# The passage between two layers of a hybrid mixer kernel, put in another order: output product by token tile, modulation and gates moved, copies shared

## Chip, cores and metric

One core of one Trainium2 chip. The metric is the device time of one execution in microseconds (us); several runs are taken and their median stands for a kernel.

## What is computed

Two trunk layers over 256 latent tokens `x` and 256 context tokens `ctx` of width 1024, float32. In each layer both streams are RMS-normalised and modulated (scale and shift from a conditioning vector), go through one wide input projection, then through three parallel token mixers (a bidirectional RWKV-7 recurrence, neighbourhood attention, differential attention), each with a SiLU gate; the branches are projected, weighted by sigmoid gates and summed, and an output projection follows. Its rows are normalised and added to the stream. In the last layer the context only serves as keys and values, so its rows need no gates and no output.

```
for l in range(DEPTH):
    mod_x = silu(c) @ w_mod[l] + b_mod[l]          # shift, scale, gate; mod_c likewise
    hx  = rmsnorm(x,  g_pre[l]) * (1 + sc_x) + sh_x
    hcn = rmsnorm(hc, g_pre[l]) * (1 + sc_c) + sh_c
    y_x, y_c = mixer(hx, hcn, w_in[l], ...)        # ends with  sum(gb * yb) @ w_out
    x  = x  + gt_x * rmsnorm(y_x, g_post[l])
    hc = hc + gt_c * rmsnorm(y_c, g_post[l])       # not in the last layer
```

## The kernel before

Tokens come in four tiles of 128: tiles 0 and 1 are `x`, tiles 2 and 3 the context. A float32 product is made of three products of float32r parts (`mm3`, high x high, high x low, low x high); weights arrive in 256 KB chunks on SP's DMA queue (`chunk`), ScalarE makes the high part `wh` and VectorE the remainder `wl` (`split`). Nearly all instructions go through helpers, so lines such as L195 (matmul), L199 (transpose), L164 (activation), L185, L189 and L192 (VectorE), L167 (DMA) stand for many places, and the tiles' names tell them apart: `z`, `a`, `b`, `y` are PSUM tags, `k` is the general pool of 52 slots of 128x512, `wr`/`wh`/`wl` weights, `gs` staging.

The order of instructions on each engine is chosen when the program is built: a scheduler goes through the program in its order as priority, with modelled durations, and emits what it takes to be ready; a slot is given when the first writer of a tile is emitted. `keep_in_program_order` pins an instruction behind everything ahead of it on its engine.

The passage from layer 0 to layer 1:

- `outproj` (L1272): for each of four column chunks `c` of 256, four weight chunks `kh`; for each, all four token tiles. When a chunk is done, each tile's PSUM is read twice: a Square on ScalarE for the norm's sum (`gs`), a product with the gate row on VectorE (`y`). `ahead` loads the old rows and, from the fifth step on, up to 15 of the 32 modulation chunks (`in_wm`).
- `residual` (L1302): one reduction and one inverse root (`rsqrt`, L201, Newton steps on VectorE) for all four tiles, then eight residual rows (L192, 128x512); tiles 0 and 1 go out to DRAM `xd` on POOL's queue, for the next layer's residual.
- `start` (L449): `norm_rows` for tiles 0 and 1, then 2 and 3 (two Squares a row, a root for each pair, scaling in place); for each of eight channel blocks `k` four transposes into `b`, a copy to `ht`. The modulation (`mod_rows`, L378) is a generator: four groups `g` of 32 small products `y<-k,cs` with 128x32 tiles, then a transpose into `z` and the scales and shifts `mA`, `mB` of two channel blocks. The loop over `g` modulates two blocks, splits them into the parts `h`, and lets weight chunks of input columns 6, 2 and 4 run on them for all 512 tokens. Then `derived` (small parameters), column chunk 0 for the x tokens, and the RWKV stage.
- `run` (L1317) weaves the recurrence (`rwkv`) with filler (`zs`: gates, further input columns) by the costs and debts in `yl`; layer 1's gates of the first branch come first in that filler.

In the RWKV stage `rwkv_inv` (L777) inverts 128 triangular blocks of 64x64: VectorE inverts the 32x32 diagonal blocks, turns the result once for each of `RA` and `RB` (`X<-X`), ScalarE copies the four turned quadrants to `Lab`, and TensorE makes the off-diagonal blocks with two passes of 32x32 products (`a<-X,Lab`, then `a<-X,k`), alternating between the two directions `d`, each direction in a block of its own of the array. It is done four times, twice in each layer.

Of the kernel before, what the change touches and what calls it, by code (L numbers as in the profile page):

```python
# [10 lines left out]
F32 = mybir.dt.float32  # L11
# [123 lines left out]
class K:  # L135
# [65 lines left out]
    def rsqrt(self, v, n, scale, eps, op=ALU.add, rows=128):  # L201

        a, b, y, t = (self.small(n) for _ in range(4))
# [158 lines left out]
    def mod_rows(self, l, P, ws):  # L362
# [9 lines left out]
        for g in range(4):  # L372
            for k in range(8):
                for i in range(4):
                    ins = self.mm(mp[32 * i:32 * i + 32, g, :], self.cs[:, k].rearrange("p a b -> p (a b)"),
                                  ws[8 * g + k][:, 128 * i:128 * i + 128], k == 0, k == 7)
# [72 lines left out]
    def start(self, l, P, xs, mod, ws, nr=T):  # L449

        self.in_order = l == 0
# [3 lines left out]
        for _ in range(8 if l == 0 else 0):  # L455
            next(mod)
# [29 lines left out]
        r = self.now(self.z_pair(l, 0, 0, nr))  # L486
        self.have["rx", l, 0] = True
        self.have["rz", l, 0] = row[0], self.rwkv_rows(l, P, 0, 1, r, 0, nr, nr == T) or [None, None], row[1]
# [288 lines left out]
    def rwkv_inv(self, e):  # L777
# [169 lines left out]
    def gates(self, l, n, b):  # L947

        for g in range(2):
# [322 lines left out]
    def outproj(self, l, s, ns, ss, ahead):  # L1272

        G = [self.gate_rows(l, st) for st in range(ns)]
        y = []
        for t in range(2 * ns):
            yt = self.k4.tile([128, 2, 512], F32, tag="k4", name=f"y{self.count()}")
            y.append([yt[:, 0, :], yt[:, 1, :]])
        for c in range(4):
            p = [self.ps("za"[c % 2], (128, 2, 256)) for _ in range(ns)]  # L1280
            for kh in range(4):
                w = self.split(self.io["wo"][l, c, kh])
                ahead(4 * c + kh)
                for t in range(2 * ns):
                    for k in range(2):
                        kk = 2 * kh + k
                        self.mm3(p[t // 2][:, t % 2, :], [a[:, 128 * t:128 * t + 128] for a in s[kk]],
                                 [a[:, k, :] for a in w], kk == 0 and t % 2 == 0, kk == 7 and t % 2 == 1)
            cs = slice(256 * (c % 2), 256 * (c % 2) + 256)
            for t in range(2 * ns):  # L1290
                pt = p[t // 2][:, t % 2, :]
                self.act(self.stage(256), pt, AF.Square, accum_out=ss[:, 4 * t + c:4 * t + c + 1])
                self.tt(y[t][c // 2][:, cs], pt, G[t // 2][c // 2][:, cs], ALU.mult)
        return y

    def rows_load(self, src, t, xs):

        xs.append([self.slot(), self.slot()])
        for j in range(2):
            self.dma(self.nc.sync, xs[t][j], src[128 * t:128 * t + 128, 512 * j:512 * j + 512])  # L1300

    def residual(self, y, ss, xs, last):  # L1302
        n = len(y)
        s2 = self.small(n)
        self.red(s2, ss.rearrange("p (t j) -> p t j", j=4), ALU.add)
        rs = self.rsqrt(s2, n, 1.0 / 1024, RMS_EPS)
        for t in range(n):
            for j in range(2):
                rows = slice(128 * t, 128 * t + 128)
# [163 lines left out]
```

## Time and profile before

| | us |
|---|---|
| median of three runs | 1433.27 |
| lowest, highest | 1431.86, 1433.60 |
| the profiled execution | 1431.83 |
| its span, first to last instruction | 1430.0 |
| mean granted TensorE clock, of full speed | 0.964 |

The profile is of one execution. Engines: PE is TensorE, PEld its weight loads, DVE VectorE, ACT ScalarE, POOL GpSimd, SP the engine that only issues DMAs here. A row of the timeline has start, duration, engine, line, operation, output<-input, count, and in brackets how long the engine was idle before and which engine and tile ended that. Ends of matmuls are modelled; the distance between starts is what they cost. PEclk 1.00 is 2.4 GHz, 0.50 the lower level of 1.2 GHz. A row of stages has the stretch and its length, busy time (and instructions) of PE, PEld, DVE, ACT and POOL, then PEclk, the busy share of the DMA engines and what they moved in GB/s.

### The profile page before, as it was taken

The page shows a single profiled execution, that of the slowest core. Times are in us where ns is not written, and L with a number is a line of the kernel's source. Part 1 is how long each engine was busy: PE and PEld are TensorE (multiplying, and loading weights), DVE is VectorE, ACT ScalarE, POOL GpSimd, SP SyncE. Part 2 cuts the span into 40 slices and gives each one's busy share as a digit, 9 for nine tenths or more (in the row PEclk, how much of TensorE's full clock was granted, in tenths as well). Part 3 has the DMA queues.
Part 4 walks back from the last instruction along what each step waited for, and adds up shares of the span by engine and source line. Part 5 has one row for each costly group of instructions (what it writes and reads, how often), then busy time and mean ns, then how long its engine had stood idle before and what let it go on. Part 6 is the DMA issues. An engine that isn't in the chain of part 4 may idle for free. (4 is left out here: it accounts for less than half of the span.)

```text
span 1430.0 us, 28585 instructions
## 1 busy us (share of the span) xinstructions
PE 1314.2 (92%) x10784; PEld 1097.1 (77%) x10784; DVE 973.4 (68%) x2047; ACT 811.5 (57%) x1750; POOL 234.6 (16%) x292
## 2 busy tenths in 40 slices
PE   6998999899998999999899969998999999989796
PEld 4865777788777876677778958887888789867686
DVE  4763469726887367768675367768837892689886
ACT  5462375545964436667533355766558736567653
POOL 0010011003110012223235001011111000022441
PEclk9999999999998999999999989999989999999998
DMA  9466642324314268422533943553613242685454
GB/s 357 125 202 191 201 137 81 118 77 143 124 62 124 64 172 236 150 97 81 199 127 122 315 156 107 186 173 115 188 61 97 75 140 69 196 266 169 130 163 148
DMA packets 112986, 212.42 MB, mean 149 GB/s; under 512 B 13088, under 2 KB 24880, under 8 KB 112848
## 3 DMA queue, kind: packets, MB, share of 16 engines
q1 hardware_dynamic: 102896, 178.33, 39.4%
q0 software_dynamic: 9952, 32.26, 6.8%
q8 instruction: 85, 1.39, 0.4%
q14 instruction: 53, 0.43, 0.1%
HBM read 176.70 MB, written 33.83 MB: 147 GB/s over the span
## 5 line engine op out<-in xcount | busy, mean ns | idle before, releaser
L195 PE MATMUL z<-k,wh 128*128 128x512 f32 (+1 forms) x2288 | 633.5, 360 | 9.5 <-ACT wh L164 5.7
L195 PEld LDWEIGHTS z<-k,wh 128*128 128x128 f32 x2288 | 406.3, 194 | 75.7 <-issue 9.4
L195 PE MATMUL z<-k,wl 128*128 128x512 f32 (+1 forms) x1144 | 408.2, 359 | 8.6 <-DVE wl L185 8.6
L164 ACT ACTIVATE wh<-wr 128x512 fp32r<-128x512 f32 x376 | 234.2, 630 | 296.8 <-PE z L195 175.9
L185 DVE TENSOR_TENSOR wl<-wr,wh 128x512 fp32r<-128x512 f32 x376 | 280.3, 752 | 170.6 <-PE z L195 70.8
L195 PEld LDWEIGHTS z<-k,wl 128*128 128x128 f32 x1144 | 221.2, 194 | 41.8 <-DVE wl L185 12.8
L195 PE MATMUL z<-wh,k 128*128 128x256 f32 x704 | 140.3, 293 | 1.5 <-ACT k L164 1.3
L195 PEld LDWEIGHTS z<-wh,k 128*128 128x128 f32 x704 | 115.5, 198 | 3.5 <-ACT k L164 1.5
L185 POOL TENSOR_TENSOR k<-k,k 64x512 fp32r<-64x512 f32 (+3 forms) x64 | 78.4, 1231 | 168.5 <-ACT k L164 88.3
L195 PE MATMUL z<-wl,k 128*128 128x256 f32 x352 | 102.7, 292 | 1.6 <-DVE wl L185 1.5
L164 ACT ACTIVATE gs<-z 128x512 f32<-128x512 f32 (+1 forms) x132 | 66.1, 501 | 63.7 <-PE z L195 54.1
L164 ACT ACTIVATE k<-k 64x256 fp32r<-64x256 f32 (+5 forms) x154 | 79.4, 541 | 29.7 <-POOL k L185 21.8
L185 DVE TENSOR_TENSOR k<-k,k 128x256 f32<-128x256 f32 (+5 forms) x126 | 79.5, 644 | 17.8 <-ACT k L164 14.6
L199 PE MATMUL b<-cst,k 128*128 128x128 f32 x384 | 67.5, 292 | 21.0 <-ACT k L164 4.8
L199 PEld LDWEIGHTS b<-cst,k 128*128 128x128 f32 x384 | 45.2, 147 | 42.5 <-issue 14.0
L164 ACT ACTIVATE k<-a,s 128x512 f32<-128x512 f32 (+1 forms) x96 | 59.1, 616 | 32.5 <-DVE s L179 31.9
L164 ACT ACTIVATE k<-b 128x256 f32<-128x256 f32 (+1 forms) x152 | 67.3, 471 | 16.9 <-PE b L199 16.0
L195 PE MATMUL a<-k,k 128*128 128x512 f32 (+1 forms) x192 | 61.0, 399 | 12.5 <-ACT k L164 10.2
L195 PEld LDWEIGHTS z<-wl,k 128*128 128x128 f32 x352 | 69.6, 198 | 2.8 <-DVE wl L185 2.3
L195 PE MATMUL a<-ar,bk 64*128 64x128 f32 (+1 forms) x512 | 49.9, 285 | 10.0 <-ACT Lab L164 9.3
L195 PEld LDWEIGHTS a<-ar,bk 64*128 64x128 f32 x512 | 42.4, 187 | 21.7 <-ACT Lab L164 16.3
L179 DVE TENSOR_REDUCE s<-a 128x1 f32<-128x512 f32 (+1 forms) x96 | 56.4, 587 | 1.7 <-PE a L195 1.7
(169 smaller groups left out, 1948.8 us busy)
## 6 DMA issues: line engine op xcount, KB each, us to landing
wr<-in_wi SPq DMA_DIRECT2D x296, 256.0 KB, 3.0
k<-in_wm SPq DMA_DIRECT2D x64, 256.0 KB, 5.4
wr<-in_wb SPq DMA_DIRECT2D x48, 256.0 KB, 2.6
md<-gs SPq DMA_DIRECT2D x36, 256.0 KB, 2.7
k<-md POOLq DMA_DIRECT2D x36, 256.0 KB, 4.3
wr<-in_wg SPq DMA_DIRECT2D x32, 256.0 KB, 2.9
wr<-in_wo SPq DMA_DIRECT2D x32, 256.0 KB, 3.9
gd<-gs SPq DMA_DIRECT2D x18, 256.0 KB, 3.0
```

Of the source, the lines that this page charges most:

```text
L164: return self.nc.scalar.activation(out=out, in_=in_, func=func, **kw)
L179: return self.nc.vector.tensor_reduce(out=out, in_=in_, axis=AX.X, op=op, **kw)
L185: return (eng or self.nc.vector).tensor_tensor(out=out, in0=a, in1=b, op=op)
L195: return self.nc.tensor.matmul(out, lhsT=lhsT, rhs=rhs, start=start, stop=stop)
L199: return self.nc.tensor.transpose(out, in_, self.ident[0:k, 0:k])
```

## The change

- `rsqrt` with one value per partition uses eight VectorE instructions in place of eleven.
- In the last column chunk `outproj` goes by token tile: all four weight chunks for tile 0, then tile 1 and so on. After each tile's reads it calls `done`, which runs residual and norm for that tile alone; in layer 0 tiles 2 and 3 are put off.
- The modulation's products stand between the projection's steps (two pieces after each step from the eighth on), their chunks are loaded earlier, and their pin is gone.
- `start_next` takes the place of `start` in layer 1: x's rows are transposed, modulated out of PSUM and split (`stream_in`), column chunk 0 and the gates of branch 0 run on the x tokens, between them the context tiles' residual and norm, then the context's stream and column chunks 6, 2 and 4.
- In `rwkv_inv` the first pass goes direction by direction, and two of the four copies to `Lab` are made by VectorE after each half of it.

```diff
     def rsqrt(self, v, n, scale, eps, op=ALU.add, rows=128):
+        if n == 1:
...
+            self.ts(t, y, y, a, ALU.mult, ALU.mult)
+            self.ts(b, t, -10.0 / 3.0, t, ALU.add, ALU.mult)
+            self.ts(y, b, 5.0, y, ALU.add, ALU.mult)
...
     def mod_rows(self, l, P, ws):
-                    if l and g == k == i == 0:
-                        self.tc.keep_in_program_order(ins)
...
+    def stream_in(self, P, hn, s):
+        c = slice(256 * s, 256 * s + 256)
+        for k in range(8):
+            p = self.ps("b", (128, 256))
+            self.turn_rows(hn, k, p)
+            t = self.slot((128, 256))
+            A, B = P["A"][:, s, k:k + 1], P["B"][:, s, k:k + 1]
+            self.ts(t, p, A, B, ALU.mult, ALU.add)
+            self.act(self.h[0][k][:, c], p, AF.Identity, scale=A, bias=B)
+            self.tt(self.h[1][k][:, c], t, self.h[0][k][:, c].bitcast(F32), ALU.subtract)
+
+    def norm_row(self, x):
+        ss = self.small(2)
+        for j in range(2):
+            self.act(self.stage(512), x[j], AF.Square, accum_out=ss[:, j:j + 1])
+        s2 = self.small(1)
+        self.red(s2, ss, ALU.add)
+        rs = self.rsqrt(s2, 1, 1.0 / 1024, RMS_EPS)
+        self.act(x[0], x[0], AF.Copy, scale=rs)
+        self.ts(x[1], x[1], rs)
+
+    def start_next(self, l, P, nr, ctx):
+        r = self.now(self.z_pair(l, 0, 0, nr))
+        self.rwkv_rows(l, P, 0, 1, r, 0, nr, False)
+        ctx[0]()
+        self.now(self.gates(l, nr, 0))
+        ctx[1]()
+        self.rwkv_wa(l, P, self.now(self.z_pair(l, 6, 0, T)), 0, T)
+        row = [self.rwkv_rows(l, P, 0, w, self.now(self.z_pair(l, c, 0, T)), 0, T, True) for w, c in ((0, 2), (2, 4))]
...
     def rwkv_inv(self, e):
+        def diag(d, q, copy):
+            R, r = RA if d == 0 else RB, rows(d, q)
+            copy(Lab[r, :, 32 * q:32 * q + 32], R[r].rearrange("p t k -> p k t"))
         for hf in range(2):
             QQ = self.ps("a", (128, 16, 32))
-            for k in range(16):
-                for d in range(2):
-                    rs, ra, cs = off(d)
-                    N = RB if d == 0 else RA
+            for d in (1, 0):
+                rs, ra, cs = off(d)
+                N = RB if d == 0 else RA
+                for k in range(16):
                     self.mm(QQ[ra, k, :], Lab[rs, 16 * hf + k, cs], N[rs, :, 16 * hf + k])
             q = self.slot((128, 16, 32))
+            self.act(q[64:96], QQ[64:96])
             self.act(q[32:64], QQ[32:64])
-            self.act(q[64:96], QQ[64:96])
             Qs.append(q)
+            diag(hf, 0, self.cp)
             yield self.yl[e["l"]]["q"][e["sg"]]
         for d in range(2):
-            R = RA if d == 0 else RB
-            for q in range(2):
-                r = rows(d, q)
-                self.act(
-                    Lab[r, :, 32 * q:32 * q + 32], R[r].rearrange("p t k -> p k t"))
+            diag(d, 1, self.act)
...
     def outproj(self, l, s, ns, ahead, done):
+            if c < 3:
+                pp = [self.ps("za"[c % 2], (128, 2, 256)) for _ in range(ns)]
+                p = [pp[t // 2][:, t % 2, :] for t in range(n)]
+            else:
+                p = [self.ps("aazz"[t], (128, 256)) for t in range(n)]
...
+            ws = []
             for kh in range(4):
+                ws.append(self.split(self.io["wo"][l, c, kh]))
                 ahead(4 * c + kh)
+                for t in range(n if c < 3 else 1):
+                    part(ws[kh], kh, t)
+            for t in range(n):
+                if c == 3 and t:
+                    for kh in range(4):
+                        part(ws[kh], kh, t)
+                read(t)
+                if c == 3:
+                    done(t, y[t], ss[t])
...
     def run(self):
                 def zs():
-                    yield from self.gates(l, nq, 0)
+                    if l == 0:
+                        yield from self.gates(l, nq, 0)
...
+                    self.derived(l + 1, PN)
+                    self.h_new()
                     mod = self.mod_rows(l + 1, PN, ws)
                 def ahead(i):
-                    if not last and i >= 4:
-                        self.mod_load(l + 1, ws, i)
+                    if not last:
+                        self.mod_load(l + 1, ws, 2 * i - 4)
+                        for _ in range(2 if i > 6 else 0):
+                            next(mod)
+                def rows(t, y, ss):
+                    self.residual(t, y, ss, xs[t], last)
+                    if not last:
+                        self.norm_row(xs[t])
+                def done(t, y, ss):
+                    if t < 2:
+                        rows(t, y, ss)
+                    else:
+                        late.append((t, y, ss))
+                self.outproj(l, s, 1 if last else 2, ahead, done)
                 if not last:
-                    next(mod)
-                self.residual(y, ss, xs, last)
-                if not last:
-                    self.start(l + 1, PN, xs, mod, ws, NX)
+                    self.mod_load(l + 1, ws, 32)
+                    self.now(mod)
+                    self.stream_in(PN, xs[0:2], 0)
+                    self.start_next(l + 1, PN, NX, (lambda: [rows(*a) for a in late],
+                                                    lambda: self.stream_in(PN, xs[2:4], 1)))
```

## Rows read from the trace of the kernel before

**Rows 1.** The page, part 1: busy time, share of the span, instructions.
```profile
PE 1314.2 (92%) x10784; PEld 1097.1 (77%) x10784; DVE 973.4 (68%) x2047; ACT 811.5 (57%) x1750; POOL 234.6 (16%) x292
```

**Rows 2.** Busy time by stage: projection, passage, part of it, after; last stage; second inversion.
```profile
786.00:823.00 37.00, 37.00 (x319) 36.87 (x321) 14.66 (x29) 13.71 (x42) 1.61 (x3) 1.00 0.89 310
822.60:846.90 24.30, 12.53 (x164) 9.01 (x162) 16.62 (x63) 15.63 (x41) 2.73 (x5) 0.72 0.43 149
...
835.00:845.00 10.00, 7.15 (x28) 4.89 (x29) 5.74 (x19) 5.74 (x10) 0.00 (x0) 0.50 0.07 26
...
846.90:884.00 37.10, 37.08 (x274) 30.31 (x275) 22.08 (x53) 15.62 (x32) 1.08 (x2) 1.00 0.38 128
...
1280.00:1430.00 150.00, 125.61 (x905) 113.47 (x904) 119.52 (x263) 85.58 (x208) 45.54 (x53) 0.94 0.49 159
458.50:474.00 15.50, 15.45 (x297) 15.07 (x298) 1.26 (x2) 12.20 (x15) 0.00 (x0) 0.64 0.12 33
```

**Rows 3.** What TensorE waited for, whole span: us in total, times, longest.
```profile
PE a L195 <- ACT k L164: 16.3, 13, 3.6
...
PE a L195 <- DVE X L182: 9.3, 3, 5.8
...
PE z L199 <- DVE k L185: 6.0, 2, 5.3
```

**Rows 4.** Groups by line and shape, 822.6 to 846.9: busy us, mean ns, idle before.
```profile
L199 PE MATMUL b<-cst,k 128*128 128x128 f32 x32 | 7.8, 415 | 4.5 <-ACT k L164 4.5
...
L164 ACT ACTIVATE gs<-k 128x512 f32<-128x512 f32 x8 | 5.0, 631 | 1.5 <-DVE k L192 1.5
...
L189 DVE TENSOR_SCALAR k<-k,mA,mB 128x256 f32<-128x256 f32 x8 | 2.9, 408 | 2.2 <-ACT k L164 2.1
...
L185 DVE TENSOR_TENSOR wl<-wr,wh 128x512 fp32r<-128x512 f32 x1 | 0.7, 691 | 0.3 <-PE a L195 0.3
```

**Rows 5.** Timeline of TensorE: transposes of the passage; a modulation group among products.
```profile
840.53 5.14 PE L199 MATMUL b<-cst,k 128*128 128x128 f32 x24 [0.47 <-ACT k L164]
...
854.99 0.39 PE L195 MATMUL b<-k,wl 128*128 128x512 f32 x1
855.31 1.95 PE L195 MATMUL y<-k,cs 128*32 128x128 f32 x64
...
857.76 0.39 PE L195 MATMUL z<-k,wl 128*128 128x512 f32 x1
```

**Rows 6.** Timeline of the projection: a weight load and products on the same rows.
```profile
821.50 0.19 PEld L195 LDWEIGHTS a<-wl,k 128*128 128x128 f32 x1
...
821.73 0.40 PE L195 MATMUL a<-wh,k 128*128 128x256 f32 x2
...
821.97 0.28 PE L195 MATMUL a<-wl,k 128*128 128x256 f32 x1
```

**Rows 7.** Tile `xd`: time of its transfers from issue to landing.
```profile
DMA to landing us min/median/max: 4.8/5.6/6.1
```

**Rows 8.** Tile `X` of the inversions: ns min/median/max, first and last start.
```profile
L195 PEld LDWEIGHTS a<-X,Lab x512: 101/121/152, 275.0 to 1183.5; 32*32 32x32 f32 x171
...
L164 ACT ACTIVATE Lab<-X x16: 1910/1942/2193, 272.7 to 1184.6; 32x1024 f32<-32x1024 f32 x16
L182 DVE STREAM_TRANSPOSE X<-X x8: 1236/1568/2151, 271.4 to 1177.9; 128x1024 f32<-128x1024 f32 x8
```

**Rows 9.** Timeline of TensorE, first inversion: its first pass of small products.
```profile
274.95 3.80 PE L195 MATMUL a<-X,Lab 32*32 32x32 f32 x128
```

**Rows 10.** Timeline of VectorE at the kernel's end.
```profile
1420.56 0.42 DVE L185 TENSOR_TENSOR y<-a,k 128x256 f32<-128x256 f32 x1 [4.36 <-ACT gs L164]
...
1421.52 0.42 DVE L185 TENSOR_TENSOR y<-a,k 128x256 f32<-128x256 f32 x1 [0.54 <-ACT gs L164]
1421.86 0.15 DVE L179 TENSOR_REDUCE s<-s 128x2 f32<-128x8 f32 x1
...
1423.83 2.74 DVE L192 SCALAR_TENSOR_TENSOR k<-y,s,k 128x512 f32<-128x512 f32 x4
```

More of the change, by code (lines that the diff above doesn't have):

```diff
@@ L201, in rsqrt @@
     def rsqrt(self, v, n, scale, eps, op=ALU.add, rows=128):
+        if n == 1:
+            a, b, y, t = (self.small(1) for _ in range(4))
+            self.ts(a, v, scale, eps, ALU.mult, op)
+            self.ts(y.bitcast(I32), a.bitcast(I32), -0.5, float(0x5F3759DF), ALU.mult, ALU.add)
+            self.ts(t, y, y, a, ALU.mult, ALU.mult)
+            self.ts(b, t, -10.0 / 3.0, t, ALU.add, ALU.mult)
+            self.ts(y, b, 5.0, y, ALU.add, ALU.mult)
+            self.ts(t, y, y, a, ALU.mult, ALU.mult)
+            self.ts(t, t, -0.5 * 0.375 ** 3, 1.5 * 0.375, ALU.mult, ALU.add)
+            self.tt(y, t, y, ALU.mult)
+            return y
         a, b, y, t = (self.small(n) for _ in range(4))
@@ L454, in start @@
         ht = []
-        for _ in range(8 if l == 0 else 0):
+        for _ in range(8):
             next(mod)
@@ L485, in start @@
         row = [self.rwkv_rows(l, P, 0, w, p[c], 0, T, True) for w, c in ((0, 2), (2, 4))]
-        r = self.now(self.z_pair(l, 0, 0, nr))
+        r = self.now(self.z_pair(l, 0, 0, T))
         self.have["rx", l, 0] = True
-        self.have["rz", l, 0] = row[0], self.rwkv_rows(l, P, 0, 1, r, 0, nr, nr == T) or [None, None], row[1]
+        self.have["rz", l, 0] = row[0], self.rwkv_rows(l, P, 0, 1, r, 0, T, True) or [None, None], row[1]
     def stage(self, n):
@@ L945, in gate_load, with gates @@
         return t
-    def gates(self, l, n, b):
-        for g in range(2):
+    def gates(self, l, n, b, gs=range(2)):
+        for g in gs:
             p = yield from self.z_pair(l, (7, 15, 23)[b] + g, 0, n)
@@ L1270, in merged, with outproj @@
         return s
-    def outproj(self, l, s, ns, ss, ahead):
+    def outproj(self, l, s, ns, ahead, done):
         G = [self.gate_rows(l, st) for st in range(ns)]
-        y = []
-        for t in range(2 * ns):
+        n = 2 * ns
+        y, ss = [], [self.small(4) for _ in range(n)]
+        for t in range(n):
             yt = self.k4.tile([128, 2, 512], F32, tag="k4", name=f"y{self.count()}")
@@ L1279, in outproj, with part, read @@
         for c in range(4):
-            p = [self.ps("za"[c % 2], (128, 2, 256)) for _ in range(ns)]
+            cs = slice(256 * (c % 2), 256 * (c % 2) + 256)
+            if c < 3:
[3 more added lines that the diff above has]
+                p = [self.ps("aazz"[t], (128, 256)) for t in range(n)]
+            def part(w, kh, t):
+                for k in range(2):
+                    kk = 2 * kh + k
+                    self.mm3(p[t], [a[:, 128 * t:128 * t + 128] for a in s[kk]], [a[:, k, :] for a in w],
+                             kk == 0 and (c == 3 or t % 2 == 0), kk == 7 and (c == 3 or t % 2 == 1))
+            def read(t):
+                self.act(self.stage(256), p[t], AF.Square, accum_out=ss[t][:, c:c + 1])
+                self.tt(y[t][c // 2][:, cs], p[t], G[t // 2][c // 2][:, cs], ALU.mult)
+            ws = []
             for kh in range(4):
-                w = self.split(self.io["wo"][l, c, kh])
+                ws.append(self.split(self.io["wo"][l, c, kh]))
                 ahead(4 * c + kh)
[L1284 to L1294, printed above, removed]
+                for t in range(n if c < 3 else 1):
+                    part(ws[kh], kh, t)
+            for t in range(n):
+                if c == 3 and t:
[4 more added lines that the diff above has]
+                    done(t, y[t], ss[t])
     def rows_load(self, src, t, xs):
@@ L1299, in rows_load, with residual @@
         for j in range(2):
[L1300 to L1309, printed above, removed]
-                xo = xs[t][j]
-                self.stt(xo, y[t][j], rs[:, t:t + 1], xo, ALU.mult, ALU.add)
-                if last:
-                    self.dma(self.nc.sync, self.out[rows, 512 * j:512 * j + 512], xo)
-                elif t < 2:
-                    self.dma(self.nc.gpsimd, self.xd[rows, 512 * j:512 * j + 512], xo)
+            self.dma(self.nc.sync, xs[-1][j], src[128 * t:128 * t + 128, 512 * j:512 * j + 512])
+    def residual(self, t, y, ss, xs, last):
+        s2 = self.small(1)
+        self.red(s2, ss, ALU.add)
+        rs = self.rsqrt(s2, 1, 1.0 / 1024, RMS_EPS)
+        for j in range(2):
+            rows = slice(128 * t, 128 * t + 128)
+            xo = xs[j]
+            self.stt(xo, y[j], rs, xo, ALU.mult, ALU.add)
+            if last:
+                self.dma(self.nc.sync, self.out[rows, 512 * j:512 * j + 512], xo)
+            elif t < 2:
+                self.dma(self.nc.gpsimd, self.xd[rows, 512 * j:512 * j + 512], xo)
     def run(self):
```

12 lines of the change are left out of this document (6 added, 6 removed).

## The prediction, made before the changed kernel was run

> **What bounds the kernel now.** I read the page's busy times first: TensorE is busy for 92% of the span, far ahead of VectorE and ScalarE [rows 1]. So time is to be had where TensorE stands idle or runs slowly, and a table of stages shows where that is. Between the last product of layer 0's output projection (822.6 us) and the first input product of layer 1 (846.9 us) it is busy for 12.5 of 24.3 us at a granted clock of 0.72, while the stages on both sides leave it no gap [rows 2]. The list of waits names what it stands for: VectorE's results `k` ahead of the modulation's turning [rows 3]; the transposes there run with a granted clock of 0.50, the lower level of 1.2 GHz, in the stretch from 835 to 845 us [rows 2]. This is the chain residual, norm, transpose, modulation; each link waits for all four token tiles.
>
> Of the 24.3 us, real work is small. Two modulation groups take 1.95 each [rows 5] (3.9). The 32 transposes took 7.8 [rows 4], nearly all at the lower level, so 3.9 at 2.4 GHz. **About 16.5 us are waste, and that is the most the passage can give.** What follows it (144 products of 512 columns, two more groups, 48 products of 256 columns) is packed and stays.
>
> **The passage, step by step.** Products of 256 columns come 0.12 apart [rows 6], so a token tile's last columns take 24 x 0.12 = 2.9, and after tile 1 (the second of the x rows) TensorE still has 5.8 us of tiles 2 and 3.
>
> Row chain of tile 1. At the kernel's end the same steps show: second read 0.96 after the first, 1.97 from the reduction to the first residual row, 0.68 per residual row [rows 10]. With one read and three inverse-root steps less (0.2 each, 1.97 over ten) the first residual starts some 2.6 us after the tile's last product. The first half goes out to `xd` at about 3.4, and the norm scales these rows in place, so it waits for that write to have landed: 5.6 more [rows 7], 9.0, and 0.7 for the scaling: 9.7. The arithmetic beside it (two squares of 0.63 [rows 4] and what reads their sums, a second inverse root of 1.8) ends at about 7.7 and is not the last; the write is, on POOL's queue, behind nothing else. Cover: 5.8 of products, and the two modulation groups left after the projection, 3.9: also 9.7. I take 1 us of idling (0 to 6).
>
> x's stream. Per 128 channels VectorE does one modulation (0.41 [rows 4]) and one subtraction (0.42, the nearest being the read in [rows 10]): 6.6 for eight, and up to two weight remainders of 0.69 [rows 4], 8. TensorE has 16 transposes (1.9) and 48 products (5.8), 7.7. With the lag at both ends 2 us idle (1 to 4).
>
> Context rows. Their residuals, norms and stream (VectorE about 16 us: four residual rows, two scalings, two inverse-root chains, 6.6 of stream, beside twelve weight remainders, 8.3, and the gates' and the first rows' own steps) have only the gates' 96 products as cover, 11.5 us, and what is done before. I take 3 (0 to 8). On SP's queue the gates' eight weight loads and two stores now stand ahead of the weights of chunks 6, 2 and 4: 2.6 MB, 8.5 us at 310 GB/s [rows 2], under 11.5 of products. A lowered clock after these gaps costs 1 (0 to 2). Waste left: 7 (1 to 20).
>
> Modulation between the projection's steps. One group among the products cost 2.77 from 854.99 to 857.76 for three products of 0.227 and 64 records at 0.0277: some 0.3 for entering and leaving [rows 5]. Eighteen pieces in nine steps instead of four groups: up to 14 x 0.3 = 4.2 more, at least nothing; I take 2.5. The passage gives 16.5 - 7 - 2.5 = **7.0** (15.5 to -8).
>
> Removed at no price: the pin of the first modulation product, the copies of the turned rows (ScalarE, off the path once the streams take their place). `derived` moves ahead of the projection: a dozen VectorE steps of 0.16 and one POOL load, under TensorE's full stage; without that cover 2 us.
>
> **The end of the kernel.** Tile 0's read, root and residual go beside tile 1's 2.9 us of products. Saved [rows 10]: a read 0.96, two residual rows 1.37, three steps 0.6. I take **2.5** (1 to 3); two output writes follow as before.
>
> **The four block inversions.** TensorE waits 9.3 us in three of them for VectorE's turned inverse [rows 3]; one turning takes 1.57 [rows 8]. The direction that needs only the first one now goes ahead, up to 1.57 each, 4.7 together. Then ScalarE spends four copies of 1.94 in a row [rows 8], and in the first inversion TensorE waits 3.6 us [rows 3] for the results queued behind them. Two go to VectorE, which is busy for 1.3 of 15.5 us in the second inversion [rows 2], so I cost them at nothing; without that cover it is 8 copies x 2 us, and the weight remainders queued behind them would make TensorE late. What is late next is ScalarE's other two copies. Gain without the reordering's price: 6 (0 to 10).
>
> The reordering's price. The small products alternate between two blocks of the array now, 3.80 us for 128 records, 29.7 ns each [rows 9]; after, sixteen in a row use one block. No row shows that. From below: transposes of 128 columns at full clock take 0.107 (an estimate: half of the 0.21 apart at which 24 of them ran at the lower level [rows 5]), 32 columns a quarter, 27 ns, so pairing hardly helps today and nothing is lost, or a little gained. From above: the load of such a block lasts 121 ns [rows 8]; if no load hides, 4 x 128 x 91 ns = 47 us. The nearest row is the projection, where loads of 0.19 us into the very rows in use lie under products 0.12 apart [rows 6], so loads do hide. I take 34 ns: 2 us in all. Net gain **4** (10 to -2, without the upper end, which is a rival).
> The Trainium skill, *TensorE: Matmul & The Clock Gate*, "The mechanism" (Part 3), speaks against this step: weight loads overlap running products only when their row groups differ. By it the sum would carry the 47 us. The trace disagrees for the whole array [rows 6] and shows nothing for one block.
>
> **Layer 1 after the passage.** The gates' 11.5 us of products are gone as filler for its recurrent part, so the interleaving draws later chunks earlier and leaves less for the attention. There TensorE is busy 125.6 and VectorE 119.5 of the last 150 us [rows 2]: filler is short. I take a loss of **1** (4, or a gain of 2).
>
> **Sum.** The profiled execution took 1431.83 (span 1430.0): 1431.8 - 7.0 - 2.5 - 4 + 1 = 1419.3. The median of the runs is 1.4 above it, so the forecast is **1421**, its own range 1412 to 1430.
>
> **Rivals.**
> *The covers all hold.* For it: both sides of the passage are packed, and the chain and its cover come out equal. Passage 13, end 3, inversions 8: 1433.3 - 24 = 1409. Against: everything must fit at once.
> *Loads become the bound.* During the projection the DMA engines are busy for 89%, at 310 GB/s, TensorE never waiting [rows 2]. The change wants 16 more modulation chunks of 256 KB by the same point, 4.2 MB, 13.5 us at that rate, against some 8 us of added TensorE time: 5.6 late; and the output weights stand behind them in SP's queue, perhaps 3 more. The passage gives nothing: 1428 to 1430.
> *Nothing moves.* The order on each engine is fixed when the program is built, from modelled times. If modulation products are put where their chunks have not landed, TensorE waits inside the projection for what it saves behind it: 1433.
> *Slower: one block at a time costs its loads.* It decides in the inversions, at the first product passes, from 29.7 ns a record: the gain is eaten at 27 ns more (14 us over 512 records), 57 ns. At 75 ns it is 1442, at the full 121 ns 1466. For it: nothing shows unpaired blocks. Against: loads under products [rows 6], and 27 ns being the stream itself.
>
> **How the numbers follow.** Forecast 0.60, covers hold 0.16, loads 0.09, nothing 0.06, slower 0.09. About 0.2% (2.9 us) is what a measurement of this kernel can tell from no change. Faster: 0.60 + 0.16 + 0.07 of the loads case = 0.83; same 0.08; slower 0.09. The range 1406 to 1432 leaves out the slower case, half of "nothing" and a few hundredths below.
>
> **What would show it.** Right: from the last projection product to the first input product of layer 1 some 8 to 12 us with two modulation groups and 16 transposes in it, TensorE's wait there naming DMA `xd` or VectorE; the stretch at the lower clock gone; at the end, two residual rows after the last product instead of four; in the inversions no 3.6 us wait, first pass 3.8 to 5 us, ScalarE two copies. Wrong: waits of TensorE or ScalarE on DMA `in_wm` or `in_wo` inside the projection; a first pass of over 7 us; the sum of idling in layer 1 after 900 us grown by more than 4.

## The result and the profile after

The changed kernel takes 1446.49 us (median of 6 runs, 1440.75 to 1448.24) beside 1432.94 for the kernel before: 1.0091 of its time, 95% interval 1.0067 to 1.0115. It is slower by 13 us where 12 less were forecast. The profiled execution took 1448.16 (span 1446.5). Part 1 of its page, against [rows 1]: TensorE has the same 10,784 records and is busy 22 us longer.

```profile
PE 1336.3 (92%) x10784; PEld 1115.0 (77%) x10784; DVE 990.9 (69%) x2109; ACT 795.3 (55%) x1742; POOL 234.9 (16%) x292
```

Where the time went is read by setting equal events of the two timelines side by side (starts, us):

| event | before | after | difference |
|---|---|---|---|
| first small products of the second inversion | 458.5 | 455.5 | -3.0 |
| second operand's wait (1.28) early in the projection | 784.9 | 788.1 | +3.2 |
| last product of the projection | 822.45 | 839.21 | +16.8 |
| layer 1's fourth group of recurrent products `a<-ar,bk` (waits 0.37 us for `Lab`) | 962.0 | 978.6 | +16.5 |
| first small products of the fourth inversion | 1179.9 | 1194.4 | +14.5 |
| last product | 1419.7 | 1437.3 | +17.6 |
| end | 1430.0 | 1446.5 | +16.5 |

So the inversions start early and end late, the projection loses 13.6 us, the stretch behind it gives nothing back (although two modulation groups, 128 records, have moved out of it into the projection), and the end gains 1.1.

**Inversions.** TensorE's timeline in the second one (start, duration, operation, count of records, idle time before):

```profile
455.54 3.82 PE L195 MATMUL a<-X,Lab 32*32 32x32 f32 x64 [5.02 <-DVE X L182]
460.44 3.81 PE L195 MATMUL a<-X,Lab 32*32 32x32 f32 x64
```

64 records of one block take 3.82 us; alternating, 128 took 3.80 [rows 9]. The starts of the single records in the two traces show more than these sums. In one block a record starts every 57 ns (median). In the alternating pass of the kernel before every second start is 57 ns after the one before last as well, and another lies in between, so that they are 28 apart on average: a block is no faster there, two blocks work side by side. The rows of tile `X` (min/median/max ns) show that the copies were no loss: ScalarE keeps eight, VectorE's eight take about half of a ScalarE copy's time. The loads' median does not tell the two orders apart: among the runs below it is 122 ns with one block at a time (`inv_only`) and 141 alternating (`pass_only`).

```profile
L195 PEld LDWEIGHTS a<-X,Lab x512: 101/141/152, 274.2 to 1201.0; 32*32 32x32 f32 x171
...
L164 ACT ACTIVATE Lab<-X x8: 1921/1952/2202, 271.9 to 1196.9; 32x1024 f32<-32x1024 f32 x8
L176 DVE COPY Lab<-X x8: 976/1022/1035, 273.7 to 1197.0; 32x1024 f32<-32x1024 f32 x8
```

**Passage.** Stages of the changed kernel (columns as in [rows 2]): the projection, a part of it, what stands in place of the old gap, and the products put ahead (the image's first input products and gates, which the change puts in front of the context's).

```profile
786.30:839.40 53.10, 47.12 (x441) 43.11 (x441) 22.23 (x71) 17.45 (x53) 5.59 (x8) 0.94 0.84 297
818.00:824.00 6.00, 5.01 (x28) 4.40 (x29) 2.24 (x6) 2.00 (x8) 0.00 (x0) 0.50 1.04 382
839.40:850.40 11.00, 7.06 (x138) 5.34 (x137) 9.40 (x41) 5.19 (x17) 1.08 (x2) 0.75 0.44 145
850.40:882.60 32.20, 25.62 (x158) 23.71 (x156) 22.75 (x64) 15.39 (x33) 0.49 (x1) 0.82 0.31 92
```

The gap of 24.3 us is 11.0 now, as forecast. But the products put ahead (144 products 0.12 apart, 17 us) take 32.2 at a granted clock of 0.82, and the projection 53.1. At the lower level such products come 0.21 apart; a clock of 0.82 is 11.6 of the 32.2 us at that level, worth up to 5 us (an estimate from these three numbers). TensorE's long waits there, from its timeline:

```profile
818.99 0.47 PE L199 MATMUL z<-cst,k 128*128 128x128 f32 x1 [4.46 <-DVE k L185]
...
843.73 0.33 PE L199 MATMUL z<-cst,k 128*128 128x128 f32 x1 [1.99 <-DVE k L185]
...
878.04 0.51 PE L195 MATMUL z<-k,wh 128*128 128x256 f32 x2 [2.83 <-DVE gs L192]
...
884.34 0.44 PE L199 MATMUL b<-cst,k 128*128 128x128 f32 x2 [1.67 <-ACT k L164]
885.90 0.69 PE L199 MATMUL b<-cst,k 128*128 128x128 f32 x2 [1.13 <-ACT k L164]
```

The first is a modulation group's turning. VectorE's timeline shows why it is late:

```profile
816.03 0.69 DVE L185 TENSOR_TENSOR wl<-wr,wh 128x512 fp32r<-128x512 f32 x1 [1.33 <-ACT wh L164]
818.04 0.69 DVE L185 TENSOR_TENSOR wl<-wr,wh 128x512 fp32r<-128x512 f32 x1 [1.33 <-ACT wh L164]
818.65 0.28 DVE L185 TENSOR_TENSOR k<-y,k 128x128 f32<-128x128 f32 x1
```

The row addition (818.65) stands behind two remainders of the last columns' weights, which wait for ScalarE's rounding, and that waits for the chunk: ScalarE stood 14.2 us for DMA `in_wo` from 786 to 840 us. In the kernel before it stood 12.1 us there, and TensorE not at all. What differs is that the last four chunks are rounded 2.0 us apart for 1.4, while the first token tile of the last columns uses one up in six products, 0.7 us. TensorE itself is at 1.2 GHz (0.50) in the stretch from 818 to 824 us, just after having stood. The wait of 2.83 us is of the same kind. VectorE's read of a gate's product (877.56) stands behind two of the context's residual rows and behind a sum that waits for ScalarE's squares:

```profile
875.08 1.42 DVE L192 SCALAR_TENSOR_TENSOR k<-y,s,k 128x512 f32<-128x512 f32 x2
877.29 0.15 DVE L179 TENSOR_REDUCE s<-s 128x1 f32<-128x2 f32 x1 [0.80 <-ACT gs L164]
...
877.56 0.42 DVE L192 SCALAR_TENSOR_TENSOR gs<-gs,z 128x256 f32<-128x256 f32 x1
```

### The profile page after: what moved, and what is told of

The parts are those of the page before. It is cut to its first block, busy times and chain, and to the rows that moved or that the text cites. A ratio compares the mean times of both kernels' runs of the same rounds, so it can differ in the third digit from the quotient of the medians.

```text
span 1446.5 us, 28636 instructions
## 1 busy us (share of the span) xinstructions
PE 1336.3 (92%) x10784; PEld 1115.0 (77%) x10784; DVE 990.9 (69%) x2109; ACT 795.3 (55%) x1742; POOL 234.9 (16%) x292
## 4 chain that ended last, share of the span: by engine, by line
PE 59%; DVE 17%; ACT 10%; DMA 7%; issue 5%; POOL 1%; SPq 1%; DVEq 0%; ACTq 0%; POOLq 0%
PE z L195 37%; PE a L195 12%; ACT k L164 6%; PE y L195 5%; DVE wl L185 4%; PE b L199 3%; DVE k L185 3%; PE b L195 3%; DMA wr<-in_wi 2%; DMA k<-in_wm 2%; DVE k L192 2%; DVE X L182 2%; ACT wh L164 1%; DVE s L179 1%; DVE X L185 1%
## 5 line engine op out<-in xcount | busy, mean ns | idle before, releaser
L195 PE MATMUL z<-k,wh 128*128 128x512 f32 (+1 forms) x2352 | 656.0, 362 | 11.4 <-ACT wh L164 5.1
L195 PEld LDWEIGHTS z<-k,wh 128*128 128x128 f32 x2352 | 419.6, 194 | 80.3 <-issue 9.2
L195 PE MATMUL z<-k,wl 128*128 128x512 f32 (+1 forms) x1176 | 422.3, 361 | 11.7 <-DVE wl L185 11.7
L195 PEld LDWEIGHTS z<-k,wl 128*128 128x128 f32 x1176 | 227.7, 194 | 47.0 <-DVE wl L185 17.0
L195 PE MATMUL z<-wh,k 128*128 128x256 f32 x736 | 148.7, 297 | 1.5 <-ACT k L164 1.3
L195 PEld LDWEIGHTS z<-wh,k 128*128 128x128 f32 x736 | 122.8, 202 | 4.3 <-ACT k L164 1.5
L195 PE MATMUL z<-wl,k 128*128 128x256 f32 x368 | 108.7, 296 | 1.7 <-DVE wl L185 1.5
L185 DVE TENSOR_TENSOR k<-k,k 128x256 fp32r<-128x256 f32 (+5 forms) x134 | 81.0, 614 | 17.8 <-ACT k L164 14.5
L164 ACT ACTIVATE k<-k 64x256 fp32r<-64x256 f32 (+5 forms) x146 | 74.7, 537 | 29.5 <-POOL k L185 21.9
L195 PEld LDWEIGHTS z<-wl,k 128*128 128x128 f32 x368 | 74.3, 202 | 2.7 <-DVE wl L185 2.3
```

The lines of the kernel that those rows point to most:

```text
L164: return self.nc.scalar.activation(out=out, in_=in_, func=func, **kw)
L185: return (eng or self.nc.vector).tensor_tensor(out=out, in0=a, in1=b, op=op)
L195: return self.nc.tensor.matmul(out, lhsT=lhsT, rhs=rhs, start=start, stop=stop)
```

## Experiments

Ratios are to the kernel before, timed together with each batch (medians 1431.38, 1432.07, 1432.61, 1433.88 and 1431.87 us); kernels of different batches are compared by them, with 0.001 taken as 1.43 us. "Stage A" is from the 1.28 us wait to the projection's last product, "stage B" from there to the fourth group of recurrent products of the table above (before: 37.5 and 139.6 us; the changed kernel: 51.1 and 139.3). Each was read in one profiled execution; where TensorE stands for nothing, stage A is 37.5 us at a granted clock of 1.00 (before, `tail_paired`) and 39.0 at 0.96 (`inv_paired`, `tiles_old`), so 1.5 us of it are the clock.

**The two halves.** `inv_only` is the kernel before with the new inversion, `pass_only` the changed kernel with the old one, and `inv_paired` and `after_paired` have the new inversion with the blocks alternating again:

```
-            for d in (1, 0):
-                ...
-                for k in range(16):
+            for k in range(16):
+                for d in (1, 0):
+                    ...
```

> The kernel before with the new block inversion alone. Theory B (one block of the array at a time makes each record of the first product pass cost 60 ns in place of 30): four first passes of 6.8 to 7.6 us in place of 3.8, partly offset by ScalarE's two copies less: 1437 to 1441. Rival (the inversion helps as forecast and the whole loss is the passage): 1427 to 1431, first passes near 4 us.

> As inv_only, but the first pass alternates between the two blocks as before; two copies on VectorE stay. Theory B: first passes back at 3.8 us, the copies' gain left alone: 1426 to 1432, 7 to 12 us under inv_only. Rival (the VectorE copies cost, not the order): within 2 us of inv_only.

> The changed kernel with the old block inversion. Theory L (16 more modulation chunks during the output projection saturate the DMA engines, so an output weight chunk comes late, VectorE stands in its queue on it, and TensorE waits for the modulation's turning): projection from its first to its last product 50 us or more in place of 39.4, and 1438 to 1444. Rival (the loss is the inversion's): 1421 to 1428.

> The changed kernel with only the alternation put back in the first pass. Theory B: 6 to 10 us under the changed kernel, 1436 to 1441, still over before by what the passage costs. Rival (order of blocks does not matter): 1445 to 1448.

`inv_only` 1439.44 us, 1.0048 (1.003 to 1.0067); `inv_paired` 1423.30, 0.9934 (0.9911 to 0.9957); `pass_only` 1442.86, 1.0082 (1.0057 to 1.0107); `after_paired` 1430.90, 0.9994 (0.9975 to 1.0013). Both halves lose. The order of the two blocks alone costs 16.1 us: shown. 512 records at 29 ns more are 14.8, and 13.0 us of it lie, in the two traces, between the first product of the first pass and the first of the second, summed over the four inversions. With it undone the inversion gains 9.5 us (0.0066 of 1432). That puts `inv_paired` below the range expected for it, as `after_paired` is, 14 us under the changed kernel by the ratios. In `inv_paired` four records run between the two turnings, the rest of the pass is as dense as before, and the wait for the results behind the copies, 3.6 us in the first inversion, is down to 1.14:

```profile
279.63 3.81 PE L195 MATMUL a<-X,k 32*32 32x32 f32 x128 [1.14 <-ACT k L164]
...
451.84 0.41 PE L195 MATMUL a<-X,Lab 32*32 32x32 f32 x4 [5.03 <-DVE X L182]
454.40 3.81 PE L195 MATMUL a<-X,Lab 32*32 32x32 f32 x124
```

The passage with the tail costs 8.6 us (0.0060) beside the paired inversion, 11.7 beside the old one. The rest is about these.

**Modulation and loads in the projection**, all from `after_paired`: `mod_late` takes the products out (`next(mod)` in `ahead` deleted), `mod_half` loads every second chunk only (it leaves out half of the modulation's weights), `turn_late` leaves the products and puts row additions and turnings behind the projection.

```
 def mod_load(...):                                    # mod_half
-    ws.append(self.chunk(...))
+    ws.append(ws[-1] if l and i % 2 else self.chunk(...))
 def mod_rows(...):                                    # turn_late
     for g in range(4):
         ...
-        row = ...; self.tt(row, ...); self.tr(...); ...
+        yield 0
+    for g in range(4):
+        yield from turn(g)
```

> The changed kernel with the two blocks' alternation restored (1430.9 us), its 32 modulation weights still loaded two to a step, but none of the modulation's products, row additions and turnings inside the projection: all of them come behind it. The length of the projection (first to last product; 39.4 us in the kernel before, about 53 us in the changed one) tells the theories apart. If the loads hold it back (the queues are full and the projection's own chunks come late), it stays at 47 to 50 us, 53 less the 4 us of products and turnings. If the turning does (TensorE waits for VectorE's row addition, which stands behind a remainder that waits for a chunk), it falls to 40 to 44 us. In the time of the whole the modulation's 8 us then stand behind the projection: 1432 to 1437 us by the loads, 1427 to 1431 by the turning.

> The same kernel (alternation restored, 1430.9 us) with every second modulation weight of layer 1 not loaded: the tile before it is read in its place, so the products, the turnings and their places are the same and the loads in the projection are half (16 of 256 KB for 32). It leaves out half of the modulation's weights. If the loads hold the projection back, it is 6 to 9 us shorter and the time 1422 to 1425 us. If the turning's wait does, there are still two of it, with the chunks less late: 1427 to 1430 us. If the stretch behind the projection takes back whatever the projection gains (VectorE's chain bounds it), 1429 to 1432.

> The same kernel (alternation restored, 1430.9 us) with the modulation's products left between the projection's steps and its four row additions and turnings behind the projection. If the turning's wait is what lengthens the projection, TensorE's longest wait for VectorE there (2.8 to 4.5 us) goes and with it the half clock that follows: 1424 to 1427 us. If the loads do, the waits come back as waits for the chunks: 1430 to 1432, and the projection stays within 2 us of what it was.

`mod_late` 1429.95 us, 0.9989 (0.997 to 1.0008); `mod_half` 1425.95, 0.9955 (0.993 to 0.9979); `turn_late` 1427.07, 0.9973 (0.9959 to 0.9987). Stage A is 50.7 in `after_paired` and 45.5, 45.6 and 45.3 in these three. With the turnings away (`turn_late`) the 32 loads cost TensorE no wait at a DMA share of 1.03 to 1.05 (785 to 815 us); with the loads halved the turnings cost none. The 5 us are lost only where both meet: a late chunk, and a turning queued behind its remainder. In `turn_late` and `mod_half` TensorE stands for only 0.2 us of stage A, so its length is TensorE's own: the old 37.5, two modulation groups (3.9) and 1.5 for the clock leave 2.4 to 2.7 for the changes of shape. `mod_late`, with none of the modulation's work in stage A, is as long for another reason. There the loads do hold TensorE up, 3.0 us in eight waits, seven of them at the first token tile of the last columns; `tiles_old` below, with the same order and the old loads, has none of them. By its length (47.3 us from first product to last) it came out as the loads' theory had it, by its time as the turning's. Its stages from 790 to 820 us, then rows of ScalarE and TensorE:

```profile
790.00:800.00 10.00, 10.00 (x86) 10.00 (x85) 2.23 (x4) 1.58 (x5) 0.00 (x0) 1.00 1.01 362
800.00:810.00 10.00, 9.39 (x76) 8.99 (x76) 2.14 (x4) 2.10 (x6) 0.00 (x0) 1.00 1.01 371
810.00:820.00 10.00, 7.58 (x40) 6.37 (x39) 5.45 (x16) 4.56 (x14) 0.00 (x0) 0.83 0.98 355
```

```profile
812.36 0.63 ACT L164 ACTIVATE wh<-wr 128x512 fp32r<-128x512 f32 x1 [1.36 <-DMA wr<-in_wo]
...
813.04 0.39 PE L195 MATMUL a<-wh,k 128*128 128x256 f32 x1 [0.42 <-ACT wh L164]
...
813.77 0.39 PE L195 MATMUL a<-wl,k 128*128 128x256 f32 x1 [0.34 <-DVE wl L185]
```

In time all three lie below `after_paired`, with intervals that overlap its own, so what stage A is worth alone is not settled to better than some 5 us. Stage B still gives little or nothing (136.9 to 139.8).

**The gates as cover.** `gates_back` has layer 1's gate products where the kernel before had them.

> The same kernel (alternation restored, 1430.9 us) with layer 1's gate products out of the passage and back among the layer's later work, where the kernel before had them; the context's rows, norms and first products stand in their order with nothing between. If the gates cover the context rows' VectorE chain, that chain now stands open: the passage keeps its 11 us less some 6 of idle time and the whole is 1434 to 1438 us. If VectorE bounds the stretch either way (the gates' own reads and the wait of 2.83 us for them go), the passage is shorter by about the gates' products and layer 1 longer by as much or less: 1427 to 1431 us.

1435.77 us, 1.0031 (1.0005 to 1.0057), 5.3 us (0.0037) above `after_paired`, with intervals that overlap, and inside the first range expected; the trace is plainer. TensorE now stands for the context's rows:

```profile
860.78 0.69 PE L199 MATMUL b<-cst,k 128*128 128x128 f32 x2 [5.31 <-ACT k L164]
866.51 0.69 PE L199 MATMUL b<-cst,k 128*128 128x128 f32 x2 [5.04 <-ACT k L164]
```

The gates do cover something. What may be wrong is the time at which the context's rows are made, and the next runs change that.

**The context's rows at once.** `ctx_now` is `turn_late`, `ctx_only` is `after_paired`, each with

```
     def done(t, y, ss):
-        if t < 2:
-            rows(t, y, ss)
-        else:
-            late.append((t, y, ss))
+        rows(t, y, ss)
```

and `turn_mid` is `ctx_now` with two turnings moved up to the first two token tiles of the last columns.

> The changed kernel with alternation and the turnings behind the projection (1427.1 us), and the context's residuals and norms done at once behind the image's, not between the products put ahead. If TensorE stands in the products put ahead because VectorE's and ScalarE's rows of the context are queued ahead of the remainders and the gates' reads (waits of 0.78, 2.1 and 2.8 us), these waits shrink and the time falls to 1421 to 1424 us. If the two engines' work in the stretch is the bound wherever it lies, the image's turning starts some 3 us later and the time is 1427 to 1431 us.

> The changed kernel with alternation (1430.9 us), its turnings still between the projection's steps, and the context's residuals and norms at once behind the image's. If the late context rows and the turnings in the projection are two losses that add, it lies as far below 1430.9 as the run with both lies below the run with the late turnings alone (1427.1 to 1417.8 us, 9 us): 1420 to 1424 us, with the projection still 50 us or more long and its wait of some 3 us still there. If the context's rows at once only help where VectorE is free of the turnings, less than 4 us go: 1427 to 1431 us.

> The run with both (late turnings, context rows at once: 1417.8 us) with the first two groups' row additions and turnings moved up to behind the first two tiles' last products of the projection, where all of its remainders have been made and nothing late is queued ahead of them. If the loss of a turning in the projection is the late chunk ahead of it on VectorE's queue, these two cost TensorE no wait, and the turning wait of 2.51 us behind the projection shrinks: 1415 to 1418 us. If a turning in the projection costs by itself (the switch of shapes, VectorE's time), 1419 to 1422 us.

`ctx_now` 1417.83 us, 0.9916 (0.9884 to 0.9949); `ctx_only` 1423.60, 0.9921 (0.9893 to 0.995); `turn_mid` 1423.35, 0.9912 (0.9886 to 0.9939). This one line is worth 0.0073 (10 us) alone and 0.0057 (8 us) beside late turnings, all of it in stage B: 131.7, 131.5 and 134.1 us for 139 to 141. Less idling of TensorE is only a part of this: in stage B it falls from 15.3 to 12.4 us (`turn_late` to `ctx_now`) and from 15.3 to 10.5 (`after_paired` to `ctx_only`). With it the granted clock of the stage rises from 0.93 to 0.96 and 0.95; how much of the time that gives back no run separates. In `after_paired` seven of the context's eight channel blocks are turned behind the gates' last product:

```profile
868.64 0.74 PE L195 MATMUL z<-k,wh 128*128 128x256 f32 x2 [2.75 <-DVE gs L192]
874.93 0.44 PE L199 MATMUL b<-cst,k 128*128 128x128 f32 x2 [1.66 <-ACT k L164]
876.50 0.69 PE L199 MATMUL b<-cst,k 128*128 128x128 f32 x2 [1.13 <-ACT k L164]
```

and in `ctx_only`, where three of the eight are turned among the gates' products, the wait of 2.75 us is gone and the last one is some 15 us earlier (the projection ends 0.9 earlier), with gate products still to come behind it:

```profile
859.97 0.44 PE L199 MATMUL b<-cst,k 128*128 128x128 f32 x2 [1.67 <-ACT k L164]
869.35 0.60 PE L199 MATMUL b<-cst,k 128*128 128x128 f32 x4
```

Once the rows are early, the turnings' place no longer shows in the time: `ctx_only` keeps a wait of 3.90 us and a stage A of 50.8, `turn_mid` and `ctx_now` have 45.5 and 45.4, and the three intervals lie on each other. `turn_mid`'s question stays open in time. In its trace the first of the two turnings does cost TensorE a wait, of 1.03 us; its stage A is no longer for that, but it ran at a clock of 1.00, where `ctx_now` had 0.96:

```profile
815.76 0.33 PE L199 MATMUL z<-cst,k 128*128 128x128 f32 x1 [1.03 <-DVE k L185]
```

**Single parts with the old passage**, on the alternating inversion: `tail_paired` has only the last layer's token tiles; `tiles_old` has them in layer 0 too, each tile's norm behind it; `tiles_out` writes the norms to new rows, and `ctx_out` does so in `ctx_now`.

```
 def norm_row(self, x):                                # tiles_out, ctx_out
-    self.act(x[0], x[0], AF.Copy, scale=rs)
-    self.ts(x[1], x[1], rs)
+    o = [self.slot(), self.slot()]
+    self.act(o[0], x[0], AF.Copy, scale=rs)
+    self.ts(o[1], x[1], rs)
+    x[:] = o
```

> The kernel before with the changed inversion (the two blocks' alternation kept, 1423.3 us) and of the passage's edits only the last layer's last columns by token tile; layer 0's projection and all that follows it as before. If the tail's gain stands by itself, as the span of the changed kernel after layer 1's last inversion has it, 2.6 us go: 1420 to 1421.5 us. If the modulation's and the norms' new places are needed for it, 1423.

> The kernel of the run before this one (tail, alternation) with layer 0's projection also ending by token tile, each tile's residual and norm right behind its products, and everything else of the passage as the kernel before has it: the modulation's loads and products in their old places, no products of the image's rows put ahead. If the passage's loss lies in the modulation's new place and in the products put ahead, and the token tiles are its good part, three tiles' residuals and norms lie under the last tiles' products and of the kernel before's 12 us of idle time behind the projection 4 to 8 go: 1413 to 1417 us. If VectorE's and ScalarE's chain of the last tile and the turning decide what the wait is, nothing goes: 1419 to 1422.

> The run with the old passage and token tiles (1428.4 us) with each tile's norm written to new rows instead of over the rows whose write to xd is still under way. If VectorE's wait of 3.51 us for that write and the tiles queued behind it are what cost it TensorE's 8.21 and 5.08 us of idling, most of these go: 1418 to 1422 us. If the chains of four tiles one after another are too long by themselves, it stays at 1425 to 1429.

> The run with late turnings and the context's rows at once (1417.8 us) with the norms written to new rows in the same way. Its trace has no wait for xd, so by either theory it stays at 1415 to 1421 us; it is there to set the two orders of the passage, both without that wait, beside each other on one chip.

`tail_paired` 1426.34 us, 0.995 (0.9931 to 0.997), not told apart from `inv_paired` and above both values expected; from last product to end it has 8.9 us for 10.3. `tiles_old` 1428.40, 0.9976 (0.9959 to 0.9992), is slower than either range expected: stage B is 147.4. VectorE's scaling of an image tile waits for the write of the rows that it overwrites, with the next tiles behind it, and TensorE behind those. VectorE's row, then TensorE's:

```profile
831.09 0.49 DVE L189 TENSOR_SCALAR k<-k,s 128x512 f32<-128x512 f32 x1 [3.51 <-DMA xd<-k]
```

```profile
838.03 0.69 PE L199 MATMUL b<-cst,k 128*128 128x128 f32 x2 [8.21 <-ACT k L164]
843.80 0.69 PE L199 MATMUL b<-cst,k 128*128 128x128 f32 x2 [5.08 <-ACT k L164]
```

`tiles_out` 1426.25, 0.995 (0.993 to 0.9971): the write's wait is gone, the time 3.7 us less (0.0026) with overlapping intervals. TensorE still stands 16.3 us, for one tile's rows after another, where it stood 15.4 for them in `tiles_old`, so most of that idling was not the write's:

```profile
825.33 0.69 PE L199 MATMUL b<-cst,k 128*128 128x128 f32 x2 [5.48 <-ACT k L164]
831.31 0.69 PE L199 MATMUL b<-cst,k 128*128 128x128 f32 x2 [5.29 <-ACT k L164]
837.03 0.69 PE L199 MATMUL b<-cst,k 128*128 128x128 f32 x2 [5.03 <-ACT k L164]
```

Four chains of about 6 us in a row are too long without products put ahead, and token tiles alone show no gain in layer 0. `ctx_out` 1429.90, 0.9979 (0.9963 to 0.9995) is a miss: 9 us lost (0.0063) where none were expected. Its stage B is 140.7 us. The new rows take slots of the pool that the modulation's chunks use; that this is the reason is argued, not shown. Six of its loads are issued at 833.73, behind the projection, where `ctx_now` has issued the last eight at 806.50; SP's queue of `ctx_out`, then of `ctx_now`:

```profile
833.73 3.18 SPq L167 DMA_DIRECT2D k<-in_wm  x6
```

```profile
806.50 5.04 SPq L167 DMA_DIRECT2D k<-in_wm  x8
```

**A version that beats both** kernels: `ctx_now`, the changed kernel with three parts put right (alternating blocks, turnings behind the projection, the context's rows at once). Its interval overlaps that of `inv_paired`, so that the passage's new order adds anything to the inversion's gain is not shown (0.0018, 2.6 us, with the tail in it).

## Why the prediction was wrong

*The inversions' order* (forecast: 34 ns a record, 2 us in all). It failed: 57 ns a record where 28 were spent before, 16 us. The lower bound, 27 ns, took the alternating pass for the bare stream of one block, "so pairing hardly helps today". But the 28 are two blocks side by side, each at 57, and one block alone leaves the other's time unused. The trace of the kernel before has this in the starts of its single records; the row of [rows 9] merges them. The choice then went by the projection's row, which has one block, the whole array, and could not show it. The slower rival had the place and the deciding point, 57 ns, and got a chance of 0.09. The rule of the Trainium skill cited there (*TensorE: Matmul & The Clock Gate*, "The mechanism") would have a load overlap only products of another row group. For the small blocks the trace agrees in sign: alternating blocks lie on different rows and go side by side, records of one block follow each other. Not in size: 29 ns a record came on top, not the 91 of the prediction's upper bound. That the load is what keeps a block at 57 ns is not shown, and for the whole array [rows 6] still speaks against the rule.

*The inversions' gain without that* (forecast 6, 0 to 10): 9.5 us. The number is inside its range, but that is in part luck. The wait for the results behind the copies went from 3.6 to 1.14 us, and VectorE's copies take 1.02 us, not the 2 of the bound: this step held. The turnings did not give 4.7: TensorE's waits for them (5.81, 1.62 and 1.90 us) became 5.03, 0.86 and 1.93, 1.5 less in all. These waits make some 4 of the 9.5 us; where the rest comes from is open.

*The passage* (forecast 7.0 less) is 8.6 to 11.7 more with the tail in it, beyond even the loss of 8 that its bounds allowed. Two steps failed. "Context rows: I take 3 (0 to 8)" was the larger: 8 to 10 us. The step priced VectorE's work against the gates' products as one sum; in the trace the order decides. Rows made between the gates' weights put remainders and gate reads behind them, and most of what needs the context (its turning) could begin only when the cover had been used up. "A lowered clock after these gaps costs 1 (0 to 2)" went wrong with it: the lower level did not go, the clock is 0.75 in the new gap and 0.82 behind it. The other is the modulation among the steps. Its 2.5 us for the change of shape came out (2.4 to 2.7) but allowed for no wait; what it left out is the row addition's place on VectorE's queue, behind remainders that wait for chunks. The wait of 4.46 us and the stretch at 1.2 GHz came with it, 5 us of stage A. The loads rival (the passage gives nothing) had half of this: without its late chunks the turning would not wait (`mod_half`). Its sign, ScalarE's waits for `in_wo`, was a poor one, as the kernel before has 12.1 us of them. The loads alone cost TensorE 3.0 us in `mod_late` and nothing in `turn_late`. The first reading held: the old gap shrank from 24.3 to 11.0 us. That its waste would not come back behind the projection was the error; stage B is 139.3 us for 139.6. Both failed steps undone (`ctx_now`), some 3 us are gained beside `inv_paired` (not clear of noise) where 9.5 were forecast for passage and end; what holds back the rest is open.

*The end* (forecast 2.5): 1.1 here, 1.4 in `tail_paired`. Two residual rows remain behind the last product as forecast. The two other savings did not come. The last tile's read starts 2.0 us after the last product, where it was 1.9, because it stands behind the first tile's residual rows on VectorE. These were to lie under the second tile's 2.9 us of products, but end 2.1 us behind them. And from the read to the first residual row it is 2.4 us for 2.3: the root with eight instructions is no faster here than the one with eleven. VectorE's rows:

```profile
1437.94 1.41 DVE L192 SCALAR_TENSOR_TENSOR k<-y,s,k 128x512 f32<-128x512 f32 x2
1439.27 0.42 DVE L185 TENSOR_TENSOR y<-a,k 128x256 f32<-128x256 f32 x1
...
1441.66 1.41 DVE L192 SCALAR_TENSOR_TENSOR k<-y,s,k 128x512 f32<-128x512 f32 x2
```

*Layer 1 later* (forecast +1): no loss is seen. From the end of stage B to the last product `after_paired` takes 455.5 us for the 453.9 of `inv_paired`, and `pass_only` 456.4 for the 457.7 of the kernel before. The pieces, by their ratios, add up as far as they were separated: -9.5 + 16.3 + 8.6 = 15.4 us, for 13.0 measured (interval 9.6 to 16.5).

## What to carry to other kernels

Before splitting a pass of small products by operand, look which blocks of the array its neighbours use, and move only the few products that have to go early. Where work is put off to lie under cover, ask what needs its result and whether that can still start under the same cover; otherwise the chain is only moved behind it. A short instruction that TensorE waits for must not be queued behind one that waits for a transfer.

## What was not expected of the hardware

- Products of 32 rows by 32 columns start every 57 ns in a block, whether it works alone (changed kernel, second inversion, granted clock 0.51) or beside another (kernel before, first inversion, 0.99). With two blocks in turn the starts are 28 ns apart on average.
- VectorE's copy of 32 by 1024 between the same tiles takes 1.02 us, ScalarE's 1.95.
- With 32 modulation loads queued the transfers move 355 to 388 GB/s at a share of 0.98 to 1.05 (`turn_late` and `mod_late`, stretches of 10 us). 16 loads more in a stage that already moves 310 cost TensorE 3.0 us of waits with no modulation products between the steps (`mod_late`) and none with them (`turn_late`).
